# Reordering the start of a one-core encoder layer: first tiles planned with a queue model of the loads, the last z and its Silu ahead of the v stage, one exponential later

## The chip, the cores and the metric

The kernel runs on one core of a Trainium2 chip. The metric is device time in microseconds for one execution. Five engines work side by side, each through its own list of instructions in order: TensorE (PE; its weight loads are shown as PEld), VectorE (DVE), ScalarE (ACT), GpSimd (POOL) and SyncE (SP), which here issues the DMAs.

## The reference

One layer of a hybrid encoder for 2048 prompt positions and 32 sample positions, width 1024, in fp32. A conditioning vector c gives, through one matrix, shifts, scales and gates ("ada" below).

```python
mod = (cs @ ada_w[l] + ada_b[l])[:, None, :]        # cs = silu(c)
sh1, sc1, gt1, sh2, sc2, gt2 = jnp.split(mod, 6, axis=-1)
h = rmsnorm(x, norm_mix_g[l]) * (1 + sc1) + sh1
p = h @ w_in                                         # columns: u, v | q, k, v | z | a, b
uv = gelu(uv); v = rmsnorm(v); a_out = u * (W_s v + b_s)
qkv = silu(causal_conv(qkv)); q, k = l2norm(q), l2norm(k)
beta = sigmoid(b); g = -exp(a_log) * softplus(a + dt_bias)
o = gated_delta_rule(q, k, v, beta, g)
b_out = rmsnorm(o, dn_norm_g) * silu(z)
x = x + gt1 * (concat(a_out, b_out) @ w_out)
x = x + gt2 * (relu(h2 @ w_up)**2 @ w_down)          # h2 as h, with sh2 and sc2
```

A last RMSNorm gives the output; the recurrent states and some rows of v go out too.

## The kernel before, in words

**Numbers.** A product in fp32 is made of three matmuls: each operand is split into a high and a low part (`wh`, `wl` of a weight; `BH`, `BL` of an activation), and the three products that matter are added in a PSUM bank. ACT makes the high part (a copy to a narrower type), DVE the low one (the difference). In the profile `wr` is a buffer for raw weights, `s` any of the general slots, `a` the scale columns of the first normalisation, `modc` the shifts. PSUM banks have tags: `g` and `L` hold products (two banks each), `C`, `B` and `M` the rest.

**Order of work.** Nothing is issued when the Python code runs: every instruction becomes an `Op` in `Program` (line 208 on) with its engine, an estimated cost, a latency, a priority (CHAIN, INV, LOCAL, EVAC, GEMM, IDLE, the first the most urgent) and the earlier operations that it depends on. `schedule` (line 248) is a list scheduler: it plays the program through with these costs (280 and 110 ns for the steps of the scale products, 1280 ns for a change of the activation table) and writes down, per engine, the order in which operations would start. A DMA is planned with a fixed latency (`LAND`, `RATE`). The chip then runs each engine's list in exactly that order and waits where an input is not there.

**Start.** `startup` (line 653 on) issues, in this order on SP: the conditioning and the constants, unit 0 of the scale matrix (`ada_load`, two loads of 512 KB), pieces of two weight slabs for z (256 KB each), and in between the tiles of x (256 KB each) and the further units of the scale matrix. PE first runs `warm` filler matmuls (`M<-ones`). `ada_first(u)` turns unit u into the scale columns of rows k = 2u and 2u + 1: eight small matmuls into a `C` bank, a copy on ACT, two matmuls of two columns, four small operations on DVE that write `a`. `scaled(0, k)` makes `BH` (ACT) and `BL` (DVE) of a tile of x; `gemm_k` then multiplies it into four z banks. `stats` squares the x tiles on ACT and gets the norm of each row; its squares wait for the products of the list `done`. Then come the second group of 512 positions, `z_shift`, the Silu of all eight z tiles (each followed by a store of 256 KB) and `h_tile`, which writes the normalised activation.

**v stage.** Sixteen tiles of the gating mixer's v follow, each of 24 matmuls into one of the two `g` banks; gelu on ACT empties a bank, and the tile after the next needs it. Steps of the modulation product (`ada`, eight matmuls into a `B` bank) and small products are slipped in between. `gates` (line 1072) needs two exponentials and a logarithm on ACT; there is a further one, `nea`, of the constant `alog`, which depends on nothing but a load. Silu, gelu and the exponential have different activation tables, and each change is an ACT_TABLE_LOAD. All of this is done for a first half of the positions and then for a second one, before the output projection and the feed-forward stage.

Of the kernel before, what the change touches and what calls it, by code (L numbers as in the profile page):

```python
# [10 lines left out]
AF = mybir.ActivationFunctionType  # L11
ALU = mybir.AluOpType
# [31 lines left out]
PE, DVE, ACT, POOL, DMA, NONE = range(6)  # L44
# [8 lines left out]


PORT = 100


CHAIN, INV, LOCAL, EVAC, GEMM, IDLE = range(6)
# [137 lines left out]
def R(x):  # L196
    return x.ap if isinstance(x, View) else x


class Op:  # L200
    __slots__ = ("eng", "cost", "lat", "fn", "npred", "succ", "prio", "hold", "slack", "table", "port", "ready", "start")

    def __init__(self, eng, cost, lat, fn, prio, table):
        self.eng, self.cost, self.lat, self.fn, self.prio, self.table = eng, cost, lat, fn, prio, table
        self.npred, self.succ, self.ready, self.start = 0, [], 0.0, 0.0


class Program:
# [39 lines left out]
    def schedule(self):  # L248

        ops = self.ops  # L250
        due = [i if o.eng == PE and o.prio == GEMM else len(ops) for i, o in enumerate(ops)]
        for i in reversed(range(len(ops))):
            due[i] = min([due[i]] + [due[j] for j in ops[i].succ])
        key = [(o.prio, due[i] if o.prio >= EVAC else i, i) for i, o in enumerate(ops)]
        free = [0.0] * 6
        port = [0.0] * 6
        wait = [[] for _ in range(6)]
        ready = [([], []) for _ in range(6)]
        table, large = None, True
        order = []  # L260

        def release(i, t):
            o = ops[i]
            if o.eng == NONE:
                finish(i, t, t)
            else:
                heapq.heappush(wait[o.eng], (t, i))

        def finish(i, start, end):
            o = ops[i]  # L270
            o.start = start
            order.append((start, i))
            for j in o.succ:
                s = ops[j]
                s.ready = max(s.ready, end + o.lat + LATENCY.get((o.eng, s.eng), 0.0) + (s.slack if o.eng != PE else 0.0))
                s.npred -= 1
                if s.npred == 0:
                    release(j, s.ready)

        for i, o in enumerate(ops):  # L280
            if o.npred == 0 and o.start == 0.0 and o.eng != NONE:
                heapq.heappush(wait[o.eng], (0.0, i))
        for i, o in enumerate(ops):
            if o.npred == 0 and o.eng == NONE and not any(k == i for _, k in order[-1:]):
                finish(i, 0.0, 0.0)
                o.npred = -1

        other = {DVE: POOL, POOL: DVE}
        while True:
            best = None  # L290
            for e in range(5):
                shared = port[other[e]] - PORT if e in other else 0.0
                t = None
                if ready[e][0]:
                    t = free[e]
                elif ready[e][1]:
                    t = max(free[e], shared)
                if wait[e]:
                    at, i = wait[e][0]
                    at = max(free[e], at, shared if ops[i].port else 0.0)  # L300
                    t = at if t is None else min(t, at)
                if t is not None and (best is None or t < best[0]):
                    best = (t, e)
            if best is None:
                break
            t, e = best
            while wait[e] and wait[e][0][0] <= t:
                i = heapq.heappop(wait[e])[1]
                heapq.heappush(ready[e][ops[i].port if e != PE else ops[i].prio == GEMM], key[i])
            shared = port[other[e]] - PORT if e in other else 0.0  # L310
            tops = [q for q in (ready[e][0], ready[e][1] if shared <= t else None) if q]
            if not tops:
                continue
            top = min(tops, key=lambda q: q[0])
            if e == PE and large and len(tops) == 2 and all(t < ops[q[-1]].ready + ops[q[-1]].hold for q in tops[0]):
                top = tops[1]
            i = heapq.heappop(top)[-1]
            o = ops[i]
            end = t + o.cost
            if e == PE:  # L320
# [12 lines left out]


class Kern:
# [61 lines left out]
    def dma(self, out, in_, n=None):  # L397
        nc = self.nc
        v = out if isinstance(out, View) else in_
        b = 4 * int(np.prod(v.shape)) if n is None else n  # L400
        x = b / 360
        self.p.op(DMA, max(500, x), lambda: nc.sync.dma_start(out=R(out), in_=R(in_)), [out], [in_], lat=LAND + b / RATE - max(500, x))

    def mms(self, calls, cost, after=()):

# [247 lines left out]
    def startup(self):  # L653
# [30 lines left out]
        k1 = self.slot(13, 512, (P, 248))  # L684
        c(k1, i["k1"])
        self.adab = k1[:, :96].re("p (j k q) -> p j k q", j=6, k=KT)
        ws = [self.ada_load(0)]
        self.cp(self.nrm, k1[:, 96:120].re("p (n k) -> p n k", n=3))
        self.cp(self.ident, k1[:, 120:248])
        self.sel = self.slot(13, 768, (P, 4))  # L690
# [8 lines left out]
        ps = [self.bank("C") for _ in range(2)]  # L699
        for e in range(2):  # L700
            self.fill(ps[e], 0.0, DVE)
        self.sq = self.slab_list()
        raws = self.raws
        self.raws = [r[:, e : e + 512] for r in raws for e in (0, 512)]
# [5 lines left out]
        zt = [[self.slot(s, lo, (P, 512)) for s in q for lo in (0, HALF)] for q in ((18, 19), (20, 27))]  # L710
        at, done = (), []
        for u in range(4):
            self.ada_first(u, ps[u % 2], ws.pop(0) if ws else self.ada_load(u), at)
            for k in (2 * u, 2 * u + 1):
                scaled(0, k)
                for h in range(H):
                    self.gemm_k(zs[h][:, :512], *z[h // 2], h % 2, 0, 0, k)
                    if h == 0:
                        done.append(last())
            at = (done[2 * u],)  # L720
        stats(0, done)
        load(1)
        for h in range(H):
            self.tt(zt[0][h], zs[h], row[0], ALU.mult)
# [5 lines left out]
        for h in range(H):  # L730
            for k in range(KT):
                self.gemm_k(zs[h][:, :512], *z[h // 2], h % 2, 0, 1, k)
            self.tt(zt[1][h], zs[h], row[1], ALU.mult)
            self.ada_first(4 + h, ps[h % 2], self.ada_load(4 + h))
        zc = self.z_shift(z)
        for g in range(2):
            o, w = GROUPS[0][g]
            for h in range(H):
                self.act(zt[g][h], zt[g][h], AF.Silu, bias=zc[:, h // 2, h % 2 : h % 2 + 1])
                self.dma(self.z_d[h][:, o : o + w], zt[g][h])  # L740
        for g in range(2):
            for k in range(KT):
# [59 lines left out]
    def ada_first(self, u, ps, ws, after=()):  # L802

        for es in ((0,), (1,)) if u < 4 else ((0, 1),):
            self.mms([(ps[32 * s : 32 * s + 2, :256], self.cs[:, 4 * e + s, :], ws[e][:, 256 * s : 256 * s + 256],
                       dict(start=(e == 0), stop=(e == 1), tile_position=(0, 32 * s), skip_group_check=True))
                      for e in es for s in range(4)], 280 * len(es), after)
            self.warm(2 if u == es[0] == 0 else 0, (len(self.p.ops) - 1,))
        self.warm((3, 4, 0, 0)[u] if u < 4 else 0, (len(self.p.ops) - 1,))
        ar = self.arow[:, 256 * (u % 2) : 256 * (u % 2) + 256]  # L810
        self.act(ar, ps[:, :256], AF.Copy)
        two = range(2 * (u % 4), 2 * (u % 4) + 2)
        for e in range(2):
# [258 lines left out]
    def gates(self, hf):  # L1072
# [963 lines left out]
```

## Time and profile before

| | before |
|---|---|
| runs, us | 2311.28, 2313.52, 2311.79 |
| median, us | 2311.79 |
| profiled execution, us | 2312.24 |
| its span, first to last instruction, us | 2310.5 |
| mean granted TensorE clock | 0.997 |
| PE, PEld, DVE, ACT, POOL busy, us | 2290.1, 2178.6, 1654.4, 1224.3, 609.3 |

Times in the profile are microseconds from the start of the span. A row of an engine shows start, duration, the source line, the operation with output and inputs, and how many such instructions were put together; a bracket gives the idle time of the engine just before it and what ended it. The source lines are mostly those of the small helpers that record an operation (L349 an activation, L364 and L369 two operations of DVE, L402 a DMA, L410 a matmul). Matmuls overlap, so their pitch, the distance of two starts, says how long one takes. The granted clock says at what share of full speed PE was allowed to run.

### The profile page before, as it was taken

To read this page: it belongs to the slowest core of one execution; us is meant where nothing else is said; L and a number is where in the kernel's file an instruction comes from. 1 tells how busy PE (TensorE), PEld (TensorE's weight loads), DVE (VectorE), ACT (ScalarE), POOL (GpSimd) and SP (SyncE) were. 2 spreads that over 40 slices of the span, in tenths; PEclk is the share of its full clock that TensorE was granted. 3 is DMA by queue.
4 is the path that set the end of the run, shared out by engine and by line. 5 is a ranking of instruction groups with operands and counts; after the bars stand their busy time and mean duration, and the time that the engine had idled before them with its cause. 6 is when DMAs were issued, how large, how long until landed. Compare 5 with 4: busy or idle time off the path is not lost.

```text
span 2310.5 us, 45792 instructions
## 1 busy us (share of the span) xinstructions
PE 2290.1 (99%) x16018; PEld 2178.6 (94%) x16018; DVE 1654.4 (72%) x3619; ACT 1224.3 (53%) x2802; POOL 609.3 (26%) x846
## 2 busy tenths in 40 slices
PE   9999999999999999999999999999999999999998
PEld 6787888999999988999999999999999999999998
DVE  5656656677754645579999989876668885666775
ACT  4655656566654434476565656754344574344344
POOL 0224532324333123344444524210000250000001
PEclk9999999999999999999999999999999999999999
DMA  8488876666566866887777787997668797666771
GB/s 313 133 266 288 260 245 211 192 204 197 186 189 181 267 199 212 279 282 252 251 255 252 266 277 255 333 319 248 213 216 259 255 304 233 219 217 218 252 220 54
DMA packets 358327, 547.08 MB, mean 237 GB/s; under 512 B 66424, under 2 KB 182284, under 8 KB 358096
## 3 DMA queue, kind: packets, MB, share of 16 engines
q1 hardware_dynamic: 358096, 544.16, 72.2%
q8 instruction: 126, 2.06, 0.4%
q14 instruction: 105, 0.86, 0.1%
HBM read 390.96 MB, written 153.05 MB: 235 GB/s over the span
## 4 chain that ended last, share of the span: by engine, by line
PE 52%; DVE 1%; issue 0%; POOL 0%; ACT 0%; POOLq 0%; DVEq 0%
PE f L410 52%; DVE s L364 0%; POOL s L364 0%; PE M L410 0%; PE M L421 0%; DVE wl L364 0%; POOLq L2032 0%; ACT wh L349 0%; ACT s L349 0%; DVEq L2032 0%; DVEq L364 0%
## 5 line engine op out<-in xcount | busy, mean ns | idle before, releaser
L349 ACT ACTIVATE s<-s 128x348 f32<-128x348 f32 (+13 forms) x1067 | 492.7, 485 | 336.9 <-DVE s L364 148.2
L410 PE MATMUL f<-s,wh 128*128 128x348 f32 (+1 forms) x2768 | 662.0, 322 | 1.5 <-ACT s L349 1.3
L410 PEld LDWEIGHTS f<-s,wh 128*128 128x128 f32 x2768 | 481.0, 188 | 3.2 <-ACT s L349 1.8
L364 DVE TENSOR_TENSOR s<-f,s 128x348 f32<-128x348 f32 (+1 forms) x696 | 347.7, 512 | 173.1 <-PE f L410 171.7
L410 PE MATMUL f<-s,wl 128*128 128x348 f32 (+1 forms) x1384 | 444.8, 321 | 0.0
L410 PE MATMUL g<-BH,wh 128*128 128x384 f32 (+2 forms) x1088 | 399.2, 367 | 3.1 <-ACT BH L349 3.1
L410 PE MATMUL g<-BH,wl 128*128 128x384 f32 (+2 forms) x1088 | 382.2, 351 | 0.0
L364 DVE TENSOR_TENSOR s<-s,s 128x348 fp32r<-128x348 f32 (+8 forms) x674 | 351.5, 550 | 42.8 <-ACT s L349 20.0
L410 PE MATMUL g<-BL,wh 128*128 128x384 f32 (+2 forms) x1088 | 381.3, 350 | 0.5 <-DVE BL L369 0.4
L410 PE MATMUL f<-BL,wh 128*128 128x348 f32 (+1 forms) x1024 | 330.2, 322 | 0.0
L410 PE MATMUL f<-BH,wh 128*128 128x348 f32 (+1 forms) x1024 | 329.4, 322 | 0.2 <-DVE s L364 0.2
L410 PE MATMUL f<-BH,wl 128*128 128x348 f32 (+1 forms) x1024 | 328.6, 321 | 0.0
L349 ACT ACTIVATE wh<-s 128x512 fp32r<-128x512 f32 x282 | 176.3, 632 | 226.3 <-PE f L410 182.1
L364 POOL TENSOR_TENSOR s<-s 64x15 f32<-64x15 f32 (+12 forms) x328 | 158.1, 482 | 451.1 <-issue 383.3
L364 POOL TENSOR_TENSOR s<-s,s 128x512 f32<-128x512 f32 (+5 forms) x153 | 195.1, 1284 | 299.0 <-ACT s L349 149.5
L410 PEld LDWEIGHTS f<-s,wl 128*128 128x128 f32 x1384 | 260.4, 188 | 0.2 <-DVE wl L364 0.2
L364 DVE TENSOR_TENSOR wl<-s,wh 128x512 fp32r<-128x512 f32 x282 | 213.9, 766 | 39.2 <-ACT wh L349 39.0
L410 PEld LDWEIGHTS g<-BH,wh 128*128 128x128 f32 x1088 | 205.1, 188 | 25.8 <-issue 5.8
L410 PEld LDWEIGHTS g<-BL,wh 128*128 128x128 f32 x1088 | 205.5, 189 | 17.8 <-DVE BL L369 1.7
L410 PEld LDWEIGHTS g<-BH,wl 128*128 128x128 f32 x1088 | 204.6, 188 | 18.2
L369 DVE SCALAR_TENSOR_TENSOR s<-s,s,s 128x256 f32<-128x256 f32 (+4 forms) x314 | 165.0, 545 | 62.2 <-ACT s L349 35.0
L410 PEld LDWEIGHTS f<-BH,wh 128*128 128x128 f32 x1024 | 192.4, 188 | 0.7 <-issue 0.5
(133 smaller groups left out, 3339.3 us busy)
## 6 DMA issues: line engine op xcount, KB each, us to landing
s<-w_u SPq DMA_DIRECT2D x124, 256.0 KB, 3.9
s<-w_d SPq DMA_DIRECT2D x121, 256.0 KB, 3.7
wh<-su_d SPq DMA_DIRECT2D x114, 256.0 KB, 3.7
wl<-su_d SPq DMA_DIRECT2D x114, 256.0 KB, 4.0
wh<-sd_d SPq DMA_DIRECT2D x100, 256.0 KB, 3.3
wl<-sd_d SPq DMA_DIRECT2D x100, 256.0 KB, 3.8
wr<-w_b SPq DMA_DIRECT2D x36, 512.0 KB, 4.7
s<-adaw SPq DMA_DIRECT2D x32, 512.0 KB, 5.2
```

The lines of the kernel that those rows point to most:

```text
L349: self.p.op(ACT, c, lambda: nc.scalar.activation(out=R(out), in_=R(in_), func=func, **{k: R(v) for k, v in kw.items()}), [out, accum], [in ...
L364: self.p.op(eng, c, lambda: e.tensor_tensor(out=R(out), in0=R(a), in1=R(b), op=op), [out], [a, b])
L369: self.p.op(DVE, c, lambda: nc.vector.scalar_tensor_tensor(out=R(out), in0=R(a), scalar=R(s), in1=R(b), op0=op0, op1=op1), [out], [a, s, b])
L410: nc.tensor.matmul(R(out), R(l), R(r), **kw)
```

## The change

1. The planner gets a queue model for loads before 30 us of plan time: a load waits for the landing of the eighth one before it, and all share one server with a fixed rate. Its landing replaces the fixed latency.
2. The loads of units 0 to 2 of the scale matrix are recorded first, `ada_first(0)` ahead of the weight slabs, then the load of unit 3: "four units of scales first". The planned cost of the scale steps goes from 280 to 620 and from 110 to 185.
3. The squares of the first group no longer wait for `done`.
4. The last multiplication of z (`zt[1]`) and all its Silus get the priority LOCAL.
5. The exponential `nea` depends on the one recorded just before it, in `gates`.

```diff
@@ schedule
+            if e == DMA and t < EARLY:
+                t = max([t] + lands[-8:-7])
+                served = max(served, t + 2330) + o.size / 310 + 50
+                lands.append(served)
+                end, o.lat = t + 430, served - t - 430
@@ startup
-        ws = [self.ada_load(0)]
+        ws = [self.ada_load(u) for u in range(3)]
...
+        self.ada_first(0, ps[0], ws[0])
+        ws.append(self.ada_load(3))
...
-            self.ada_first(u, ps[u % 2], ws.pop(0) if ws else self.ada_load(u), at)
+            if u:
+                self.ada_first(u, ps[u % 2], ws[u], at)
...
-        stats(0, done)
+        stats(0, ())
...
-            self.tt(zt[1][h], zs[h], row[1], ALU.mult)
+            with self.p.at(LOCAL):
+                self.tt(zt[1][h], zs[h], row[1], ALU.mult)
...
-                self.act(zt[g][h], zt[g][h], AF.Silu, bias=zc[:, h // 2, h % 2 : h % 2 + 1])
+                with self.p.at(LOCAL):
+                    self.act(zt[g][h], zt[g][h], AF.Silu, bias=zc[:, h // 2, h % 2 : h % 2 + 1])
@@ ada_first
-                      for e in es for s in range(4)], 280 * len(es), after)
+                      for e in es for s in range(4)], 620 * len(es), after)
...
-            self.mm(ps[:, 256 + 2 * e : 258 + 2 * e], ar[:, 128 * e : 128 * e + 128], self.sel[:, 0:2], 110)
+            self.mm(ps[:, 256 + 2 * e : 258 + 2 * e], ar[:, 128 * e : 128 * e + 128], self.sel[:, 0:2], 185)
@@ gates
-            self.act(self.nea, self.alog, AF.Exp)
+            self.act(self.nea, self.alog, AF.Exp, after=(len(self.p.ops) - 1,))
```

What the planner makes of it shows in the engines' lists. **First place: the first z products.** ACT before, from its first weight split on (`wr_96` raw pieces of the first z slab, `s_492` the first piece of the second, `s_475` the first two x tiles, `C_498` the scales of unit 0):

```order
L349 ACTIVATE wh<-wr_96 128x512
L349 ACTIVATE s_480<-C_498 128x256
L349 ACTIVATE wh<-s_492 128x512
L349 ACTIVATE wh<-wr_96 128x512
L349 ACTIVATE BH_71<-s_475,a_89 128x512
```

ACT after, from the same split on:

```order
L358 ACTIVATE wh<-wr_96 128x512
L358 ACTIVATE s_480<-C_498 128x256
L358 ACTIVATE s_491<-s_475 128x512
L358 ACTIVATE wh<-s_492 128x512
L358 ACTIVATE BH_71<-s_475,a_89 128x512
```

The split of the second piece of the first slab stood ahead of the first `BH` and now stands behind it; a square (`s_491`) came in before. PE before, from the first z product on (`g_504`, `g_505`, `L_506` three of the four z banks, `C_499` the bank of scale unit 1, whose two halves are `s_469` and `s_470`):

```order
L410 MATMUL g_504<-BH_71,wh 128x512
L410 MATMUL g_504<-BL_79,wh 128x512
L410 MATMUL g_504<-BH_71,wl 128x512
L410 MATMUL g_505<-BH_71,wh 128x512
L410 MATMUL g_505<-BL_79,wh 128x512
L410 MATMUL g_505<-BH_71,wl 128x512
L410 MATMUL C_499<-s_469,s_484 2x256 x4
L410 MATMUL L_506<-BH_71,wh 128x512
```

PE after, from the same product on:

```order
L420 MATMUL g_504<-BH_71,wh 128x512
L420 MATMUL g_504<-BL_79,wh 128x512
L420 MATMUL g_504<-BH_71,wl 128x512
L420 MATMUL C_499<-s_469,s_484 2x256 x4
L420 MATMUL g_505<-BH_71,wh 128x512
L420 MATMUL g_505<-BL_79,wh 128x512
L420 MATMUL g_505<-BH_71,wl 128x512
L420 MATMUL L_506<-BH_71,wh 128x512
```

The first half of scale unit 1 moved ahead of three z products; on SP its two loads moved from the eleventh and twelfth place to the ninth and tenth, ahead of the second weight piece.

**Second place: the first tiles of the v stage.** ACT before (`s_494` and `s_487` z tiles under Silu, `g_1015` the first v tile under gelu, then the tiles after it):

```order
L349 ACT_TABLE_LOAD
L349 ACTIVATE s_485<-g_1015 128x256
L349 ACTIVATE BH_75<-s_474 128x512
L349 ACTIVATE s_489,s_484<-s_485 128x256
L349 ACTIVATE s_485<-g_1070 128x256
L349 ACTIVATE s_489,s_484<-s_485 128x256
L349 ACTIVATE BH_77<-s_479 128x512
L349 ACTIVATE s_479<-s_479,modc,a_89 128x512
L349 ACT_TABLE_LOAD
L349 ACTIVATE s_494<-s_494,s_480 128x512
L349 ACT_TABLE_LOAD
L349 ACTIVATE s_485<-g_1205 128x256
```

ACT after, from the last Silu on:

```order
L358 ACTIVATE s_494<-s_494,s_480 128x512
L358 ACT_TABLE_LOAD
L358 ACTIVATE s_485<-g_1015 128x256
L358 ACTIVATE s_489,s_484<-s_485 128x256
L358 ACTIVATE s_479<-s_479,modc,a_89 128x512
L358 ACTIVATE BH_77<-s_479 128x512
L358 ACTIVATE s_485<-g_1075 128x256
L358 ACTIVATE BH_78<-s_479 128x512
L358 ACTIVATE s_489,s_484<-s_485 128x256
L358 ACTIVATE s_485<-g_1210 128x256
```

The last Silu moved from behind the second v tile's gelu to ahead of the first one's, and the two table loads around it are gone. Two more, around the exponential `nea` (`s_484<-s_484 128x4`) among the first Silus, are gone as well; over the whole program ACT's list has 35 table loads before and 37 after.

**Third place: the twelfth to fourteenth tile of the v stage.** On ACT the row is the same in both, the gelu of the eleventh tile, a square, a weight split (`wh<-wr_96 128x1024`), a table load, the exponential, a table load, the gelu of the twelfth tile (`g_1535` before, `g_1524` after). PE before, from the end of the twelfth tile on (`B_1016` the modulation product, `g_1563` the thirteenth tile):

```order
L410 MATMUL g_1535<-wl,BH_78 128x260
L410 MATMUL g_1535<-wh,BL_86 128x260
L410 MATMUL B_1016<-s_467,s_484 2x512 x2
L410 MATMUL B_1016<-s_468,s_484 2x512 x2
L410 MATMUL B_1016<-s_469,s_484 2x512 x2
L410 MATMUL B_1016<-s_474,s_484 2x512 x2
L410 MATMUL g_1563<-wh,BH_71 128x260
```

PE after, from the end of the twelfth tile on:

```order
L420 MATMUL g_1524<-wl,BH_78 128x260
L420 MATMUL g_1524<-wh,BL_86 128x260
L420 MATMUL g_1572<-wh,BH_71 128x260
L420 MATMUL g_1572<-wl,BH_71 128x260
L420 MATMUL g_1572<-wh,BL_79 128x260
```

The modulation step moved from between these two tiles into the eleventh one (`g_1488`); the next one after stands near the end of the fourteenth tile (`g_1632`), which needs the bank of the twelfth. In the second half of the positions a weight split, a table load, the exponential, a table load and a gelu stand in the same way behind a v tile (`g_4826`, `g_4920`), and of the steps that PE had there between the two tiles one of four matmuls is left; the feed-forward stage has the same order in both kernels.

More of the change, by code (lines that the diff above doesn't have):

```diff
@@ L55 @@
 PORT = 100
+EARLY = 30000
 CHAIN, INV, LOCAL, EVAC, GEMM, IDLE = range(6)
@@ L200 @@
 class Op:
-    __slots__ = ("eng", "cost", "lat", "fn", "npred", "succ", "prio", "hold", "slack", "table", "port", "ready", "start")
+    __slots__ = ("eng", "cost", "lat", "fn", "npred", "succ", "prio", "hold", "slack", "table", "port", "ready", "start", "size")
     def __init__(self, eng, cost, lat, fn, prio, table):
@@ L205, in __init__ @@
         self.npred, self.succ, self.ready, self.start = 0, [], 0.0, 0.0
+        self.size = 0
 class Program:
@@ L259, in schedule @@
         table, large = None, True
-        order = []
+        order, served, lands = [], 0.0, []
         def release(i, t):
@@ L402, in dma @@
         self.p.op(DMA, max(500, x), lambda: nc.sync.dma_start(out=R(out), in_=R(in_)), [out], [in_], lat=LAND + b / RATE - max(500, x))
+        self.p.ops[-1].size = b
     def mms(self, calls, cost, after=()):
```

## The prediction

> **What bounds the kernel now.** I read the page first, then busy time by stretches of the span, then PE's waits, then the instructions of PE, ACT and DVE one by one where a wait stood.
>
> The page's first lines:
>
> ```profile
> span 2310.5 us, 45792 instructions
> PE 2290.1 (99%) x16018; PEld 2178.6 (94%) x16018; DVE 1654.4 (72%) x3619; ACT 1224.3 (53%) x2802; POOL 609.3 (26%) x846
> ```
>
> PE is busy for 99% of the span, so a change in order can only win back PE's idle 20.4 us (2310.5 - 2290.1) and time in which PE is busy at a lower clock. Where these lie, the windows show (stretch, its length, then busy time and count of PE, PEld, DVE, ACT, POOL, then PE's granted clock, the DMA engines' share and GB/s):
>
> ```profile
> 0.00:20.00 20.00, 14.46 (x83) 10.57 (x84) 8.11 (x24) 6.67 (x11) 0.20 (x4) 0.91 0.88 302
> 20.00:40.00 20.00, 19.83 (x123) 14.18 (x122) 13.54 (x28) 13.32 (x25) 0.00 (x0) 1.00 1.00 373
> 80.00:100.00 20.00, 17.55 (x131) 15.85 (x133) 11.44 (x21) 15.02 (x27) 1.15 (x2) 0.93 0.26 80
> 160.00:220.00 60.00, 60.00 (x287) 44.47 (x286) 42.40 (x62) 33.06 (x53) 31.10 (x38) 1.00 0.91 305
> ```
>
> Two of these stretches are loose: the first lacks 5.5 us of PE and the one from 80 us lacks 2.45 us, and in both the clock is below 1. PE's waits name one cause for each (engine, line, who was waited for: us, times, longest):
>
> ```profile
> PE g L410 <- ACT BH L349: 3.1, 1, 3.1
> PE g L410 <- ACT s L349: 2.5, 1, 2.5
> ```
>
> **The start.** PE, then ACT, then DVE (start, duration, instruction, and in brackets the idle time before it and who ended it):
>
> ```profile
> 10.06 1.58 PE L410 MATMUL M<-ones 128*128 128x128 f32 x12
> 14.74 0.51 PE L410 MATMUL g<-BH,wh 128*128 128x512 f32 x1 [3.09 <-ACT BH L349]
> 15.52 0.80 PE L410 MATMUL g<-BL,wh 128*128 128x512 f32 x1 [0.28 <-DVE BL L369]
> 16.97 0.63 PE L410 MATMUL g<-BL,wh 128*128 128x512 f32 x1
> 17.40 0.63 PE L410 MATMUL g<-BH,wl 128*128 128x512 f32 x1
> 17.96 1.04 PE L410 MATMUL C<-s,s 128*2 128x256 f32 x8
> 18.92 0.50 PE L410 MATMUL L<-BH,wh 128*128 128x512 f32 x1
> 19.26 0.39 PE L410 MATMUL L<-BL,wh 128*128 128x512 f32 x1
> 19.49 0.40 PE L410 MATMUL L<-BH,wl 128*128 128x512 f32 x1
> ```
>
> ```profile
> 8.64 0.63 ACT L349 ACTIVATE wh<-wr 128x512 fp32r<-128x512 f32 x1 [6.06 <-DMA wr<-w_b]
> 10.08 0.63 ACT L349 ACTIVATE wh<-s 128x512 fp32r<-128x512 f32 x1 [0.54 <-DMA s<-w_b]
> 13.44 0.63 ACT L349 ACTIVATE wh<-wr 128x512 fp32r<-128x512 f32 x1 [2.73 <-DMA wr<-w_b]
> 13.98 1.32 ACT L349 ACTIVATE BH<-s,a 128x512 fp32r<-128x512 f32 x2
> ```
>
> ```profile
> 10.74 0.69 DVE L364 TENSOR_TENSOR wl<-s,wh 128x512 fp32r<-128x512 f32 x1 [0.75 <-ACT wh L349]
> 14.72 1.42 DVE L369 SCALAR_TENSOR_TENSOR BL<-s,a,BH 128x512 fp32r<-128x512 f32 x2
> ```
>
> The fillers end at 11.64 (10.06 + 1.58). The first z matmul needs BH; BH stands on ACT behind a weight split that waits until 13.44 for a load it has nothing to do with. After the idle 3.09 us the matmuls come every 0.43 us (16.97, 17.40); from 18.92 on they come every 0.23 (19.26, 19.49): half clock. So the wait costs twice.
>
> With the new order, BH runs right behind the split that ends at 10.71 (10.08 + 0.63): 0.66 us (half of 1.32) to 11.4, under the fillers. DVE's wl ends at 11.43; one scale column and BL (0.71, half of 1.42) bring it to about 12.35. So PE starts at 11.64 instead of 14.74, does its second matmul at 12.35 instead of 15.52, and has the first three behind it at about 12.85 (two more at 0.23).
>
> There a new wait can stand: the next instruction takes the second unit of scales, which the old order took at 17.96. Its first half is now the load in the place of the weight piece that landed at 13.44, and is twice as large. Latest: 13.44 + 256 KB at the 302 GB/s of the first window (0.87) = 14.3. Earliest: behind the piece that landed at 10.08 come 768 KB at the 373 GB/s of the second window (2.1) = 12.2. The middle, 13.25, gives a wait of 0.4 (0 to 1.45). Queued behind it on PE are nine z matmuls. They then take 0.3 for the scale step and 0.7 for three matmuls: what before had done at 18.92 is done at about 14.25, 4.67 us earlier, if no half clock follows so short a wait. I take **4.3**: a few tenths are left for the second half of that unit and for the weight pieces, which now land later by the 1 MB put ahead of them. Low end: a wait of 1.45 (1.05 more) and again half clock, whose price is 20% of the stretch's matmuls, (0.43 - 0.23) for some nine matmuls = 1.8: 4.67 - 2.85 = 1.8. High end 4.7.
>
> The squares that no longer wait for `done` cost ACT 0.6 each, in gaps where it waits for loads; the planner's larger costs for scale steps are no work.
>
> **The start of the v stage.** PE, then ACT:
>
> ```profile
> 93.12 0.28 PE L410 MATMUL g<-wh,BL 128*128 128x260 f32 x1
> 95.86 0.39 PE L410 MATMUL g<-wh,BH 128*128 128x260 f32 x1 [2.45 <-ACT s L349]
> 97.41 0.42 PE L410 MATMUL g<-wh,BH 128*128 128x260 f32 x1
> 97.63 0.42 PE L410 MATMUL g<-wl,BH 128*128 128x260 f32 x1
> 101.62 0.39 PE L410 MATMUL g<-wh,BH 128*128 128x260 f32 x1
> ```
>
> ```profile
> 92.10 1.28 ACT L349 ACT_TABLE_LOAD   x1
> 93.39 0.72 ACT L349 ACTIVATE s<-s,s 128x512 f32<-128x512 f32 x1
> 94.13 1.28 ACT L349 ACT_TABLE_LOAD   x1
> ```
>
> The last Silu of z stands between two table loads, its own and the one back to gelu, while PE waits for gelu to empty a bank. From 97.41 the pitch is 0.22 where it is 0.12 at full clock: half clock again. Dense, 18 matmuls at 0.12 (2.16) and a modulation step of 1.83 (128.26 to 130.09, rows below) would go from 93.24 to 97.23; they went to 101.62. The change has all Silus ahead of the first gelu, and the early exponential no longer stands among them: **4.4** comes back. What is late next is gelu itself, at 0.38 and a square of 0.42 per 2.88 us of tile (24 x 0.12): no wait. The stores of z go out earlier, into a stretch with a DMA share of 0.26.
>
> **The exponential's tables.** ACT and then PE at the twelfth tile:
>
> ```profile
> 128.36 1.06 ACT L349 ACTIVATE wh<-wr 128x1024 fp32r<-128x1024 f32 x1 [1.76 <-PE g L410]
> 129.44 1.28 ACT L349 ACT_TABLE_LOAD   x1
> 130.73 0.26 ACT L349 ACTIVATE s<-s 128x32 f32<-128x32 f32 x1
> 131.01 1.28 ACT L349 ACT_TABLE_LOAD   x1
> 132.30 0.38 ACT L349 ACTIVATE s<-g 128x256 f32<-128x256 f32 x1
> ```
>
> ```profile
> 128.26 1.90 PE L410 MATMUL B<-s,s 128*2 128x512 f32 x16
> 130.09 0.39 PE L410 MATMUL g<-wh,BH 128*128 128x260 f32 x1
> ```
>
> This ACT piece is kept, with a weight split that starts when PE ends a tile. The gelu of that tile is done 4.3 us later (132.68 - 128.36), and the tile after the next needs its bank. Before, PE had the modulation step (1.83) and a tile (2.88) to do, 4.7 us: covered. After, that step stands a tile earlier and PE has 2.88 alone: from 128.16 it would be through at 131.04, and the bank is free at about 132.74. **-1.7.** Queued behind it on PE is everything else.
>
> The trace has 0.02 us between a table's load and its neighbours (129.42 to 129.44, 130.72 to 130.73), and the sum goes by that. The Trainium skill ("ScalarE: Activation LUTs", What ACT_TABLE_LOAD costs) adds a drain of about 1.38 us to each switch and speaks against this change: by it the stall would be some 2.8 us longer, an estimate, and the time 2308.3. The trace disagrees.
>
> **The second half** has the same pattern: a weight split, two loads and the exponential between a tile and its gelu, with four short matmuls in place of a step and more. By the rows above the new stall is at most the same 1.7. One wait of before may go in exchange:
>
> ```profile
> 397.29 1.13 PE L410 MATMUL M<-s,s 128*128 128x128 f32 x8 [1.10 <-DVE s L364]
> ```
>
> So between -1.7 and +1.1; I take **-0.7**, nearer to the stall.
>
> **Sum.** 4.3 + 4.4 - 1.7 - 0.7 = 6.3. The profiled run took 2312.24 (1.74 around its span); 2305.9 on that basis. The median of the runs is 0.45 below it: **2305.5**.
>
> **Rivals.**
>
> Half clock after the new stall. Idle stretches of 3.09 and 2.45 us were followed by half clock, that of 1.10 at 397.29 was not; 1.7 lies between. The price is what it cost at 97.41: 4.39 - 2.45 - 0.2 = 1.7, so 2307.2. The Trainium skill ("TensorE: Matmul & The Clock Gate", What's actually happening) asks for an idle window of about 3.4 us; by it this rival falls away and 2305.5 stays. The trace disagrees, since 2.45 us sufficed. Chance 0.15.
>
> The loads do not come as planned: the second unit lands at 14.3 and the change does not do at the start what its queue model says. Gain there 1.8 instead of 4.3: 2308.0. For it: the first window moved only 302 GB/s. Against it: the load takes one place earlier in any case. Chance 0.10.
>
> The gain is given back: PE asks for everything 8.7 us earlier, and from 160 to 220 us the DMA share is 0.91. If the weights there arrive when they did, PE waits and the end stays: 2311.8. Against it: PE does not wait once in these 60 us. Chance 0.12.
>
> Neither new stall appears, because other work slips in: 6.3 + 2.4 = 8.7, 2303.1. Chance 0.13.
>
> Slower: the tables. The whole program loads
>
> ```profile
> L349 ACT ACT_TABLE_LOAD x35 | 44.9, 1283 | 1.3 <-PEq L2029 0.7
> ```
>
> and the changed order 37; four go at the v stage, so six come elsewhere. If each stalls PE by its 1.28 and draws half clock behind it (1.7), 6 x 3.0 = 17.9 stand against 8.7: 2321. It decides from (8.7 + 4.6) / 6 = 2.2 us per load. Against it: of PE's waits, the two quoted are the longest, and only one of them has table loads in it, two of the 35. Chance 0.05.
>
> **Numbers.** The forecast as worked has 0.45. A measurement of this kernel can tell about 0.2% from no change, 4.6 us: faster is below 2307.2, slower above 2316.4. Faster: 0.45, the case without stalls 0.13, and half of the half-clock case (0.08): 0.66. Same: the other half of it, the late loads, the gain given back: 0.29. Slower: 0.05. The range reaches down to 2302.8, just past the case without stalls, and up to 2309.0, past half clock and late loads; left out are the gain given back and the tables, 0.17.
>
> **What would show it.** Right: first z matmul at about 11.7, no pitch of 0.43 between 12 and 20 us, one table load before the v stage's first gelu, no 2.45 us wait, a wait of about 1.7 us on ACT at the fourteenth v tile. Wrong: a wait of over 1 us for the second unit of scales; pitches of 0.22 in the v stage; new waits for weights between 160 and 220 us; waits of PE behind table loads in the second half that add to over 3 us.

## The result, and the profile after

Over twenty runs of each kernel the changed one takes 2310.11 us (median; 2307.26 to 2312.91) and the kernel before 2313.34 us (2310.94 to 2315.54). The ratio is 0.9987 with a 95% interval of 0.9981 to 0.9993: 3.2 us faster, with 1.6 to 4.4 in the interval. That is about half of the 6.3 us that were forecast. The time itself lies 1.1 us above the stated range, and part of that is the base: the three runs that the prediction had show a median of 2311.79, 1.55 us below that of the twenty. By the prediction's own measure of 0.2% (4.6 us) the change counts as "same", to which it gave 0.29.

The profiled execution of the changed kernel took 2309.89 us. Its page:

```profile
span 2308.1 us, 45801 instructions
PE 2289.0 (99%) x16018; PEld 2176.4 (94%) x16018; DVE 1662.3 (72%) x3619; ACT 1224.4 (53%) x2804; POOL 599.6 (26%) x846
```

The windows (columns as in the prediction) that answer to those of before, and the stretch of the new wait:

```profile
0.00:20.00 20.00, 16.55 (x109) 12.53 (x110) 9.50 (x30) 8.55 (x15) 0.20 (x4) 1.00 0.87 307
...
80.00:100.00 20.00, 20.00 (x171) 18.23 (x173) 7.61 (x21) 8.39 (x23) 1.32 (x3) 1.00 0.46 155
...
120.00:140.00 20.00, 18.46 (x152) 16.47 (x151) 9.34 (x37) 9.98 (x24) 1.62 (x3) 1.00 0.69 235
...
160.00:220.00 60.00, 60.00 (x299) 45.04 (x298) 42.10 (x68) 35.02 (x63) 25.71 (x38) 1.00 0.88 301
```

PE is busy for 2.1 us more by 20 us, has no hole and full clock at the start of the v stage, a new hole of 1.54 us between 120 and 140, and again none between 160 and 220. The kernel before had no hole between 120 and 140:

```profile
120.00:140.00 20.00, 20.00 (x169) 18.35 (x169) 6.24 (x22) 9.78 (x22) 1.08 (x2) 1.00 0.64 222
```

**The start.** PE, then ACT:

```profile
12.53 0.49 PE L420 MATMUL g<-BH,wh 128*128 128x512 f32 x1 [0.93 <-ACT BH L358]
13.49 0.50 PE L420 MATMUL g<-BL,wh 128*128 128x512 f32 x1 [0.47 <-DVE BL L378]
...
14.16 0.61 PE L420 MATMUL C<-s,s 128*2 128x256 f32 x8
14.70 0.50 PE L420 MATMUL g<-BH,wh 128*128 128x512 f32 x1
...
15.51 0.39 PE L420 MATMUL L<-BH,wh 128*128 128x512 f32 x1
```

```profile
10.57 0.63 ACT L358 ACTIVATE s<-s 128x512 f32<-128x512 f32 x1 [1.08 <-DMA s<-xT]
11.24 0.63 ACT L358 ACTIVATE wh<-s 128x512 fp32r<-128x512 f32 x1
11.77 1.32 ACT L358 ACTIVATE BH<-s,a 128x512 fp32r<-128x512 f32 x2
```

The square that came in ahead of the weight split waits 1.08 us for its x tile, so `BH` starts at 11.77 and not at 10.71, and PE starts on z at 12.53 and not at 11.64. On the other side, PE does not wait at 14.16 for the second unit of scales. The first `L` product starts at 15.51 instead of 18.92: 3.4 us earlier, where the forecast had 4.7, and there is no half clock.

**The v stage.** ACT at its first gelu:

```profile
79.40 0.71 ACT L358 ACTIVATE s<-s,s 128x512 f32<-128x512 f32 x1
80.13 1.28 ACT L358 ACT_TABLE_LOAD   x1
81.42 0.39 ACT L358 ACTIVATE s<-g 128x256 f32<-128x256 f32 x1
```

The last Silu is over before the one table load; no other follows among the first tiles.

**The exponential's tables.** ACT at the twelfth tile, then PE at the fourteenth, at its counterpart in the second half, and in a later stage:

```profile
121.87 1.06 ACT L358 ACTIVATE wh<-wr 128x1024 fp32r<-128x1024 f32 x1 [1.76 <-PE g L420]
122.95 1.28 ACT L358 ACT_TABLE_LOAD   x1
124.25 0.26 ACT L358 ACTIVATE s<-s 128x32 f32<-128x32 f32 x1
124.53 1.28 ACT L358 ACT_TABLE_LOAD   x1
125.82 0.66 ACT L358 ACTIVATE s<-g 128x256 f32<-128x256 f32 x2
```

```profile
126.26 0.39 PE L420 MATMUL g<-wh,BH 128*128 128x260 f32 x1 [1.54 <-ACT s L358]
126.48 0.28 PE L420 MATMUL g<-wl,BH 128*128 128x260 f32 x1
...
432.96 0.39 PE L420 MATMUL g<-wh,BH 128*128 128x260 f32 x1 [0.94 <-ACT s L358]
...
687.56 0.71 PE L420 MATMUL C<-s,s 128*128 128x128 f32 x4 [0.29 <-DVE s L378]
```

The wait that was forecast as 1.7 us is there with 1.54, and no half clock behind it (PEclk is 1.00 from 120 to 140).

**Where the gain goes.** PE does the same work in both kernels, in another order, so I compare at equal work: each PE instruction counts the median distance to the next one of its kind over all profiles of this case, idle time left out; at each sum of this work, the table has the time in the profile of before minus the time in the other, so a positive number is a lead. These are differences of single executions:

```
us of PE work          30    75   100   160   350   480   760  1020  2200
changed kernel       3.95  4.23  8.53  6.46  6.01  5.20  3.91  3.80  2.39
changed, again (e10) 4.09  4.38  8.67  6.60  6.20  4.77  3.94  3.48  1.63
before, again (e12) -0.66 -0.66  0.92  0.92  0.93  1.09  0.97  1.00  0.18
```

The sums of work are a model. Without it the lead can be read where both kernels have issued the same set of PE instructions: it is 8.4 us at 102 us of the profile of before, 6.6 at 164, 5.2 at 486, 3.9 at 773 and 2.5 at the end (8.6, 6.7, 4.7, 3.9 and 1.8 in e10), within 0.2 of the table.

At 100 us the changed kernel is 8.5 us ahead, as the first two terms of the forecast say (8.7). Then it loses: 2.1 at the fourteenth tile, 1.3 to 1.8 more up to 480, about 1 up to 760, and 1.5 to 2.3 in the rest.

### The profile page after: what moved, and what is told of

Same layout as the page of the kernel before. It is cut to its first block, busy times and chain, and to the rows that moved or that the text cites. A ratio compares the mean times of both kernels' runs of the same rounds, so it can differ in the third digit from the quotient of the medians.

```text
span 2308.1 us, 45801 instructions
## 1 busy us (share of the span) xinstructions
PE 2289.0 (99%) x16018; PEld 2176.4 (94%) x16018; DVE 1662.3 (72%) x3619; ACT 1224.4 (53%) x2804; POOL 599.6 (26%) x846
## 4 chain that ended last, share of the span: by engine, by line
PE 49%; DMA 1%; DVE 1%; ACT 1%; issue 1%; POOL 0%; POOLq 0%; DVEq 0%; SPq 0%; ACTq 0%
PE f L420 49%; DVE s L373 1%; ACT s L358 1%; DMA s<-r_d 0%; DMA th_d<-s 0%; DMA yT<-s 0%; DMA wl<-sd_d 0%; DMA s<-w_d 0%; DVE wl L373 0%; POOL s L373 0%; DMA s<-w_u 0%; PE M L420 0%; PE M L431 0%; ACT wh L358 0%; DVE s L378 0%
## 5 line engine op out<-in xcount | busy, mean ns | idle before, releaser
L373 DVE TENSOR_TENSOR s<-s,s 128x348 fp32r<-128x348 f32 (+7 forms) x674 | 353.4, 553 | 47.8 <-ACT s L358 25.3
L373 POOL TENSOR_TENSOR s<-s,s 128x512 f32<-128x512 f32 (+5 forms) x153 | 190.4, 1252 | 302.0 <-ACT s L358 151.4
```

The lines of the kernel that those rows point to most:

```text
L373: self.p.op(eng, c, lambda: e.tensor_tensor(out=R(out), in0=R(a), in1=R(b), op=op), [out], [a, b])
```

## The experiments

Theory 1: the gain of the first 100 us is real and stays; what is lost later is the fault of the later order of instructions, which the planner laid out anew although the change is about the start. Theory 2: a head start is given back later whatever the order. To tell them apart, some kernels take the order from a list instead of the planner. They record what the changed kernel records; `A` and `B` are the planner's orders of the changed kernel and of before, with its start times `tA` and `tB`:

```diff
-            for o in self.p.schedule():
-                o.fn()
+            for i in written():
+                self.p.ops[i].fn()
```

Each was timed beside the kernel before on its chip (2312.41 us in the first four, 2312.65 in the next, 2312.93 in the last). The work table for them, against the first profile of before:

```
us of PE work          30    75   100   160   350   480   760  1020  2200
e1 head              4.08  4.37  8.66  8.52  8.52  8.75  8.99  9.52  9.19
e2 tail             -1.60 -1.60 -0.02 -3.12 -3.86 -4.71 -5.49 -5.14 -5.82
e3 exp behind        2.16  2.44  6.74  5.65  4.86  3.11  0.89  0.80 -0.26
e4 start             3.96  2.81  2.85  2.85  2.86  3.16  3.25  3.33  2.27
e5 v part           -0.87 -0.89  3.32  3.41  3.41  3.07  2.98  3.57  2.75
e6 start part        3.47  3.76  7.68  5.65  5.24  5.11  4.65  5.50  3.41
e7 step              0.14  0.15  1.73 -0.99 -0.99 -0.86 -0.94 -0.15 -0.29
e8 old costs         2.94  2.00  6.23  6.31  6.31  6.37  6.74  6.71  5.72
e9 mid               3.05  3.34  7.63  5.56  4.96  3.78  4.05  4.08  2.93
e11 head, again      1.88  2.16  6.45  6.35  6.35  6.55  6.33  7.13  6.17
```

**e1: the head of the changed order, the rest of before.** `T` is the start of the eleventh v tile.

```diff
+S = {i for i in A if tA[i] < T}
+order = [i for i in A if i in S] + [i for i in B_with_nea_in_its_new_place if i not in S]
```

> The changed kernel's order up to the start of the eleventh v tile (all of the start, all Silus ahead of the first gelu), and the order of the kernel before for everything behind it (with the exponential nea kept at its new, later place). Theory 1, the head start of about 8.5 us that the changed kernel has at that tile is kept, and what it lost later is the fault of the order behind it: 8 to 9 us below the kernel before, ratio about 0.9963, no wait at the fourteenth v tile. Theory 2, a head start is given back later whatever the order, since loads or other engines set the pace there: 3 to 4 us below the kernel before, as the whole change.

Measured: 2304.37 us, ratio 0.9965 (0.9952 to 0.9977), 8 us below the kernel before. Its page, its windows, and its table loads:

```profile
span 2301.4 us, 45792 instructions
...
PE 2286.1 (99%) x16018; PEld 2177.3 (95%) x16018; DVE 1659.4 (72%) x3619; ACT 1218.6 (53%) x2798; POOL 605.0 (26%) x846
```

```profile
0.00:20.00 20.00, 16.69 (x109) 12.65 (x110) 9.62 (x30) 8.68 (x16) 0.20 (x4) 1.00 0.87 305
80.00:100.00 20.00, 20.00 (x170) 18.14 (x172) 7.60 (x22) 8.28 (x22) 1.32 (x3) 1.00 0.47 153
...
120.00:140.00 20.00, 19.96 (x162) 16.66 (x155) 11.31 (x42) 14.14 (x29) 2.38 (x5) 1.00 0.71 229
```

```profile
L358 ACT ACT_TABLE_LOAD x31 | 39.8, 1283 | 1.3 <-PEq L2435 0.7
```

No wait at the fourteenth tile, and the 8.66 us of 100 are still 9.19 at the end. Theory 2 falls.

**e2: the other half.**

```diff
+S = {i for i in B if tB[i] < T_of_B}
+order = [i for i in B if i in S] + [i for i in A if i not in S]
```

> The other half: the order of the kernel before up to the start of the eleventh v tile, and the changed kernel's order behind it. Theory 1: the order behind that tile costs about 5 us by itself, so 5 us above the kernel before, ratio about 1.0022, with a wait of about 1.5 us at the fourteenth v tile. Theory 2: the same as the kernel before within 1 to 2 us.

Measured: 2318.07 us, ratio 1.0026 (1.0015 to 1.0036), 5.7 us slower. PE's waits:

```profile
PE g L420 <- ACT s L358: 4.9, 3, 2.5
PE g L420 <- ACT BH L358: 4.0, 1, 4.0
```

The three waits on ACT are the old 2.45, the new 1.54 and the 0.94 of the second half. By the work table the later order costs 5.8 us, from -0.02 at 100 to -5.82; the start's wait was 4.0 in this execution, which adds 1.6; the start of the v stage gets them back, since full clock follows the 2.45 here.

**e3: the exponential behind the thirteenth tile's gelu.** Operations of the changed order moved:

```diff
 gelu of tile 12
-(ahead of it: table load, exponential of the gates, table load)
 gelu of tile 13, squares
+exponential of the gates (and the five DVE operations that use it)
```

> The changed kernel with one thing moved: the exponential of the gates and what DVE makes of it stand behind the gelu and square of the thirteenth v tile instead of ahead of the gelu of the twelfth. Theory 1: the wait of 1.54 us at the fourteenth tile goes and nothing takes its place, so 1.5 us below the changed kernel, 4.7 below the kernel before, ratio about 0.9980. Theory 2: the wait goes but turns up again before the feed-forward stage, so as the changed kernel, 3.2 below the kernel before.

Measured: 2309.46 us, ratio 0.9987 (0.9978 to 0.9995): 3 us below before (1.2 to 5.1 by the interval), so no difference from the changed kernel that can be told. The number is that of theory 2, but the interval holds the 4.7 of theory 1 as well. The wait at the fourteenth tile is gone, but a product that needs the gates waits in its place, on PE:

```profile
131.60 1.16 PE L420 MATMUL M<-s,s 128*128 128x128 f32 x8 [0.75 <-DVE s L378]
```

From 100 to 160 us of work the kernel loses 1.1 instead of 2.1. It then loses 4.8 up to 760 where the changed kernel loses 2.6, although PE's order is the same, and half clock at its start cost 1.8. One microsecond of 2310 cannot be settled this way; the run tells nothing for either theory.

**e4: the start alone.**

```diff
+S = {i for i in A if tA[i] < end_of_first_group_of_z}
+order = [i for i in A if i in S] + [i for i in B if i not in S]
```

> Only the first part: the changed kernel's order up to the end of the first group's z products, then the order of the kernel before, with its two table loads and its wait at the start of the v stage. Theory 1: the 4.2 us that the changed kernel is ahead at the first v tile are kept, 4.2 below the kernel before, ratio about 0.9982. Theory 2: 1 to 2 us below the kernel before.

Measured: 2310.15 us, ratio 0.9989 (0.998 to 0.9998), 2.3 us below. The first of these windows shows why it is less than 4.2, the second the old hole and half clock at the v stage:

```profile
40.00:60.00 20.00, 18.72 (x190) 11.57 (x188) 13.17 (x25) 8.33 (x18) 7.00 (x12) 1.00 0.80 287
80.00:100.00 20.00, 17.55 (x133) 15.16 (x132) 8.91 (x17) 12.43 (x24) 0.50 (x2) 0.91 0.26 81
```

At the seam between the two orders PE waits 1.2 us that neither order has. The 2.81 that are left at 75 us are still there at 350.

**e5: the last two edits alone, by the planner.**

```diff
+            with self.p.at(LOCAL):
+                self.tt(zt[1][h], zs[h], row[1], ALU.mult)
...
+                with self.p.at(LOCAL):
+                    self.act(zt[g][h], zt[g][h], AF.Silu, bias=zc[:, h // 2, h % 2 : h % 2 + 1])
...
-            self.act(self.nea, self.alog, AF.Exp)
+            self.act(self.nea, self.alog, AF.Exp, after=(len(self.p.ops) - 1,))
```

> The kernel before with the last two edits alone (the priority of the last z and its Silus, and the later exponential); the planner lays out the rest. It leaves PE's order behind the v stage nearly as before, with the modulation step inside the thirteenth v tile. Theory 1 (what the whole change lost came from an order that its other edits brought): the 4.3 us of the v stage's start are kept to the end, ratio 0.9981, no wait over 0.3 us between 100 and 380 us. Rival (an earlier v stage makes PE wait for something later): 1 to 2 us gained, ratio 0.9993.

Measured: 2309.07 us, ratio 0.9985 (0.9977 to 0.9994), 3.6 us below. Its window at the start of the v stage:

```profile
80.00:100.00 20.00, 20.00 (x156) 17.83 (x155) 13.76 (x28) 13.87 (x29) 3.01 (x4) 1.00 0.25 78
```

The work table has 4.2 gained from 75 to 100 (-0.89 to 3.32; 2.6 against the second profile of before, e12) and all of it still there at 350 (3.41). Two edits out of five bring as much as the whole change.

**e6: the changed kernel without them.** The lines of e5 go back to those of before, and the rest of the change stays:

```diff
-            with self.p.at(LOCAL):
-                self.tt(zt[1][h], zs[h], row[1], ALU.mult)
+            self.tt(zt[1][h], zs[h], row[1], ALU.mult)
...
-            self.act(self.nea, self.alog, AF.Exp, after=(len(self.p.ops) - 1,))
+            self.act(self.nea, self.alog, AF.Exp)
```

> The changed kernel without the last two edits: queue model, order of the loads, free squares and larger costs alone. Its order behind the v stage is close to the changed kernel's, with the modulation step in the eleventh tile again. Theory 1: 4.2 us ahead at the first v tile, the wait of 2.45 us and half clock at the start of the v stage as before, then the 5 us of the later order lost: 0 to 2 us above the kernel before, ratio 1.0000 to 1.0009. Rival (the start's gain is kept): 4 us below, ratio 0.9982.

Measured: 2309.14 us, ratio 0.9987 (0.9978 to 0.9996), 3.5 us below. Theory 1's number missed. The later loss is there (7.68 at 100, 3.41 at the end, with the wait of 1.54), but the hole at the start of the v stage, on which I counted, is not:

```profile
80.00:100.00 20.00, 19.91 (x165) 18.05 (x164) 7.69 (x20) 14.94 (x29) 1.27 (x3) 1.00 0.52 171
```

The last two Silus still stand between gelus there, but apart, each with its own pair of table loads between two tiles, and PE does not wait for one pair. So the hole depended on a detail of the order that other edits change as well. The two parts, e5 and e6, bring 3.6 and 3.5 us alone and 3.2 together.

**e7: the modulation step moved, in the order of before.**

```diff
+order = B with the modulation step between tiles 12 and 13 moved into tile 11
```

> The kernel before with one operation of PE moved: the modulation step between the twelfth and the thirteenth v tile stands in the eleventh instead, as in the changed kernel. This is the new wait by itself. Theory 1: a wait of 1.5 to 1.7 us at the fourteenth tile and some 0.5 us of pitch, 2 us above the kernel before, ratio 1.0009, no half clock behind it. Rival (half clock behind the wait in some executions): up to 3.7 us above, ratio 1.0016.

Measured: 2314.5 us, ratio 1.0012 (1.0003 to 1.0021), 1.9 us slower. The wait at the fourteenth tile is 1.54 again, with full clock behind it. A part came that neither theory had; the step on PE:

```profile
121.12 2.81 PE L420 MATMUL B<-s,s 128*2 128x512 f32 x16
```

At its old place it took 1.90. Moved ahead it runs before its loads are in: the weight loads of PE wait 0.45 and 0.83 us in it. In the changed kernel it does not pay this.

**e8: the old planned costs.** One edit of the change undone:

```diff
-                      for e in es for s in range(4)], 620 * len(es), after)
+                      for e in es for s in range(4)], 280 * len(es), after)
...
-            self.mm(ps[:, 256 + 2 * e : 258 + 2 * e], ar[:, 128 * e : 128 * e + 128], self.sel[:, 0:2], 185)
+            self.mm(ps[:, 256 + 2 * e : 258 + 2 * e], ar[:, 128 * e : 128 * e + 128], self.sel[:, 0:2], 110)
```

> The changed kernel with one edit undone: the planned costs of the scale steps are 280 and 110 again. The start is the same but for one small matmul, and PE's order behind the v stage is then nearly that of the kernel before, with 31 table loads. Theory 1, now narrower (the larger costs are what tips the later order into a worse one): 8 to 9 us below the kernel before, ratio 0.9963. Rival (the later loss comes from the earlier start): 3 us below, as the changed kernel.

Measured: 2306.38 us, ratio 0.9973 (0.9963 to 0.9983), 6.3 us below the kernel before. Its table loads and its window:

```profile
L358 ACT ACT_TABLE_LOAD x31 | 39.8, 1283 | 1.3 <-PEq L2044 0.7
```

```profile
120.00:140.00 20.00, 20.00 (x166) 16.61 (x166) 10.47 (x37) 12.33 (x28) 2.17 (x4) 1.00 0.65 212
```

From 100 to 1020 us of work nothing is lost (6.23 to 6.71). The start lost about 1 us more than in the changed kernel and there is a wait of 1.1 at 46 us; that is what it lacks to 8. With all other edits in place, the larger costs alone decide which later order comes out: by the names in the traces, PE's order here is that of the kernel before from 125 us on, and in the changed kernel only from 909 us on.

**e9: the changed order up to the end of the second half's v stage.**

```diff
+S = {i for i in A if tA[i] <= end_of_second_v_stage}
+order = [i for i in A if i in S] + [i for i in B if i not in S]
```

> The changed kernel's order up to the end of the second half's v stage (about 465 us), the order of the kernel before behind it. Theory 1: the changed kernel is some 5.3 us ahead there, and what it lost from there to the output projection (1.4 us by its profile) goes with its order: 5 us below the kernel before, ratio 0.9977, and by the profile no loss over 0.3 us between 480 and 760 us of work. Rival (that loss has nothing to do with the order): as the changed kernel, 3 us below, with a loss of over 1 us in that stretch.

Measured: 2307.89 us, ratio 0.998 (0.9971 to 0.9989), 5 us below. PE's waits have the two of the v tiles still:

```profile
PE g L420 <- ACT s L358: 2.5, 2, 1.5
```

Up to 480 us it loses as the changed kernel does (7.63 to 3.78), and from 480 to 760 it loses nothing (3.78 to 4.05) where the changed kernel loses 1.3 and 0.8. That part of the loss lies in the order too, though only 0.8 us of waits show there in the first profile; the rest is pitch.

**e10: the changed kernel again.** No edit.

> The changed kernel once more, for a second profile on the same chip as the others of this call. Theory 1: again a wait of 1.54 us at the fourteenth v tile, 0.94 us at its counterpart in the second half, and a loss of 0.5 to 1.5 us between 480 and 760 us of work, since they are in the order; the loss in the feed-forward stage differs by over 0.5 us from the first profile's 1.4, since that is chance. 3 us below the kernel before.

Measured: 2309.86 us, ratio 0.9989 (0.998 to 0.9998), 3.1 us below. The waits of 1.54 and 0.94 are there, 0.8 is lost between 480 and 760, and in the feed-forward stage (1020 to 2200) 1.85 against 1.41. That differs by 0.44 and not by over 0.5, so this comparison does not show that this part is chance.

**e11: the first experiment's kernel again.** No edit.

> The first experiment's kernel once more, on one chip with the changed kernel. Theory 1: 8 us below the kernel before and 5 us below the changed one. Rival (the first run was lucky): 5 to 6 us below the kernel before.

Measured: 2306.26 us, ratio 0.9971 (0.996 to 0.9982), 6.7 us below, between the two expectations. In this profile half clock followed the start's waits of 1.14 and 0.47 us, and it is 2.2 us less ahead at 30 us than e1 (1.88 against 4.08); nothing is lost from 100 to 1020. It is 3.6 us faster than the changed kernel on one chip. No other order has a lower ratio than its two (0.9965 and 0.9971), but e8 with 0.9973 cannot be told from them.

**e12: the kernel before again.** No edit.

> The kernel before once more, for its profile. If half clock behind a wait depends on where the wait falls, as the runs so far suggest, the waits of 2.45 us at the v stage and of some 3 us at the start are there again to 0.3 us, and half clock may or may not follow the first. If it depends on the wait's length alone, it follows both again.

Measured: 2312.4 us, ratio 0.9997 (0.9988 to 1.0006). PE at the start of the v stage, and its window:

```profile
96.52 0.39 PE L410 MATMUL g<-wh,BH 128*128 128x260 f32 x1 [2.45 <-ACT s L349]
...
97.47 0.28 PE L410 MATMUL g<-wl,BH 128*128 128x260 f32 x1
97.59 0.28 PE L410 MATMUL g<-wh,BL 128*128 128x260 f32 x1
```

```profile
80.00:100.00 20.00, 17.55 (x137) 15.90 (x140) 12.11 (x22) 15.68 (x28) 1.55 (x3) 1.00 0.24 74
```

The same wait of 2.45 us, and the matmuls behind it at a pitch of 0.12, full clock. So the 1.6 us that half clock cost here in the first profile is not in every execution.

## Why the prediction was wrong

**The start, 4.3: size right, in part by luck.** The changed kernel is 4.2 and 4.4 ahead at 75 us in its two profiles. The way there was not as worked out: `BH` came 1.1 us later, since the square in front of the split waits for x, which I had put down as filling a gap; the scales' wait of 0.4 did not come, but the scale step takes 0.54 us (14.16 to 14.70) and not 0.3. At the first `L` product the lead is 3.4 and not 4.7. It then grows by 0.5 up to 30 us and 0.3 up to 75, where the forecast had a few tenths lost. (Half clock costs 0.20 us for each matmul there, 0.43 - 0.23; the "20%" is a slip, and the 1.8 stands.)

**The start of the v stage, 4.4: mechanism right, size too large.** One execution had it. The hole of 2.45 us is in all five profiles that have the old order there (before, e2, e4, e7, e12), but half clock follows in two only (before, e4). From 75 to 100 us the changed kernel gains 4.3 on the first profile of before and 2.7 on the second. With two in five, an estimate from few executions, that is 2.7 + 0.4 x 1.6 = 3.3, some 1 us less than the term. And the gain did not need these two edits: e6 has it without them.

**The fourteenth tile, -1.7: right.** The wait is 1.54 in all six profiles with that order (the changed kernel, e2, e6, e7, e9, e10), and half clock followed none of them, so that rival did not happen. The loss there is somewhat more than the wait, 2.1 by the work table and 1.9 at equal instructions; that the tile split around the moved step makes the rest is not shown by itself.

**The second half, -0.7: too small.** The 1.10 us at 397 went down to 0.4 or less, as the better end of the term had it, but the new wait of 0.94 came with 0.42 more at 466 us and with pitch: 1.3 to 1.8 from 160 to 480.

**What failed is the edit that was costed at nothing, and beside it the size of the v stage's term.** The prediction says that "the planner's larger costs for scale steps are no work". They are none, but they decide the order of work for hundreds of microseconds behind them: without them (e8) the loss from 100 to 1020 us is gone. I had looked at the places where the order differed and PE could wait, and priced two of them. I gave no term to the rest of the new order, between 480 and 760 us, which cost about 1 us, mostly without a wait that a list of waits would name. By the two profiles of each kernel, with the 3.3 worked out above for the v stage, the parts make 3.2 us at 760: 4.6 for the start (at 75 us the changed kernel's mean is 4.3, that of before -0.3), 3.3, then -2.1, -1.6 and -1.0. So of the 3.1 us that the forecast of 6.3 has too many, the later order accounts for 2.3 (4.7 lost where 2.4 were priced) and the v stage for 1.1, less 0.3 that the start brought more.

Why the new order has a longer pitch between 160 and 760 us stays open: e8 and e9 show that the loss goes with the order, and not what in it costs.

**What stays open** is also the rest, from 760 us on. The changed kernel's two profiles lose 1.5 and 2.3 there, the second one of before 0.8, e1 none, e8 1.0. By the names in the traces, the two kernels have the same order on all five engines from 957 us on, and at equal instructions none of this is lost before 1000 us (the lead is 3.9 at 773 and 4.1 at 1009 us in both profiles of the changed kernel). So the order behind 957 us is not its cause; executions of one order scatter there by about as much as the difference. The runs give 3.2 us for the whole, with 1.6 to 4.4 in the interval, which the sum at 760 fits with or without such a loss.

**The other rivals.** The gain given back in the loads' stretch from 160 to 220 us did not happen: no wait there, and e1 keeps all. The case without stalls is what e1 and e8 are (ratios 0.9965, 0.9971 and 0.9973), and it would have come without the larger costs. Six more table loads than in e1 and e8 (37 against 31) are there, but the waits they were feared for are not: PE's longest waits on ACT between the start of the v stage and 1000 us, 1.54 and 0.94, came at two pairs of loads that the kernel before has as well, covered there. Whether the other loads have a part in the longer pitch is not shown.

## What to carry to other kernels

Where a list scheduler lays out the whole program, an edit at its start changes the order to its end: price the places where the new order differs, or hold the rest of the order fixed while trying the edit, as e1 does; that alone was worth more here than the change. A planner's cost is not free because it is no work: move each number by itself and look at what it moves. And one profile's half clock behind a short wait is no price for every execution; count it by how often it shows.

## What the runs showed of the hardware

The same wait does not bring half clock in every execution. Behind 2.8 to 4.0 us at the start it came in all five profiles with the old start; behind 2.45 us at the v stage in two of five; behind the two waits at the new start (0.5 to 1.6 and 0.3 to 0.5 us) in two of nine (e3, e11); behind 1.54 us in none of six.

The clock records of the traces show in part why. In each execution the recorded changes of the granted clock lie on a grid of 3.41 us; half clock at these places lasts one or two of its steps (3.41 or 6.83 us), and the grid lies differently against the work each time. By its rows PE was, at the new start, idle for 1.43 (e3) and 1.61 us (e11) within one step where half clock followed, and for at most 1.36 in the seven others. Of the 2.45 us at the v stage, 1.89 (before) and 2.40 (e4) fell within one step where half clock followed, and 1.68 (e7), 1.84 (e2) and 1.87 (e12) where it did not. One threshold does not fit both places, so how a step is judged is not shown. The Trainium skill ("TensorE: Matmul & The Clock Gate", What's actually happening) has a free-running window of about 3.4 us, which fits that the same wait goes either way, but asks for a whole idle window, and 2.45 us were enough here.

A table load is 1.28 us and its neighbour starts 0.01 us behind it (124.53 + 1.28 = 125.81, then 125.82). The median of this distance is 0.01 us in each of the fourteen profiles, so no drain follows a load here.
